# Six held pieces: when the long convolution's matmuls may be queued among the heads of the second mixer's attention

## The chip, the cores and the metric

One core of one Trainium2 chip runs the whole program. The metric is the device time of one execution in microseconds (us): 2259.91 us for the kernel before, the median of three runs (2259.61 to 2260.74). About 0.2% of it, 4.5 us, is what a measurement of this kernel can tell from no change.

## The reference, cut to what matters

The program is three transformer-like blocks in a row over 512 positions of width 1024. Only the middle of the second block is touched. There, one projection feeds two branches that don't depend on each other until their outputs are projected and added:

```
q = rope(rmsnorm(q)); k = rope(rmsnorm(k))            # 8 heads of 96
w = softmax(q @ k.T * 96**-0.5)                       # 512 x 512 per head
y_attn = w @ v                                        # 8 heads of 64

x0, x1, vh = split(dwconv3(u_h))                      # 3 x 512 channels
u = x1 * vh
y = irfft(rfft(u, 1024) * rfft(kcirc, 1024))[:512] + u * bias
y_hyena = x0 * y

x = x + concat(rmsnorm(y_attn), rmsnorm(y_hyena)) @ w_out
```

The kernel does the two transforms as matmuls with constant cosine and sine matrices. All large matmuls are done in three passes of split operands (high times high, low times high, high times low), so each weight tile is first cast to its high part on ScalarE and its low part is made by a subtraction on VectorE.

## The kernel before

The function is `mix2`. The position axis (512) is four tiles of 128. The program is written as one straight trace; a planner then orders it at compile time: it walks a simulated time line, lets every engine take the ready instruction that stands earliest in the trace, and fixes by that the order of each engine's queue. On the chip every queue runs in that order. Work that stands late in the trace but is ready early therefore fills holes of the work before it.

What stands where, in the order of the trace:

- Eight projections for the convolution's `x1` and `vh` (`uh`), with the norms of the attention's q and k between them, and the four products `us[i]`. `turned(i)` turns each product with four TensorE transposes into a bank of the tag `t`, and empties that bank by four pairs of a ScalarE copy (line 1484) and a VectorE subtraction (line 1485).
- `rotate` of q (lines 1375 to 1377), then `gate0(0)` and `gate0(1)`: each one projection of 24 matmuls and a three-tap convolution (line 268, 1283, 1285, 1286), stored for later. Then `turned(3)`.
- The attention. `heads(hd)` turns q and then k of one head (line 1582), into one `t` bank each, and empties the banks on ScalarE (line 211) and VectorE (line 212). `scores(hd)` makes four score tiles of three matmuls each in the two banks `s`, takes the row maximum on VectorE (line 1597) and the exponential on ScalarE (line 1599) into one of five buffers `P`. `values(hd)` turns the four `P` tiles, 16 transposes (line 1612, copied out by line 1614), and in every second head multiplies with v in the bank `o` and scales by the inverse sums.
- The six pieces of the list `fill`: `gate0(2)`, `gate0(3)`, `forward(0)`, `forward(1)`, `inverse(0)`, `inverse(1)`. A `forward` has 24 matmuls of 512 columns, mirrors them (lines 1273 to 1275), multiplies with the stored filter spectrum (lines 1526 to 1531 on VectorE and GpSimd), adds and subtracts (1535, 1536, GpSimd) and splits four results (202 and 204). Its eight buffers of the tag `tmp` are all that there are. An `inverse` has 48 matmuls of 256 columns and reads all eight split results of both forwards; then come line 1562 on VectorE, 1563 on GpSimd, and a split (211, 212).
- `hyena(n)`, eight output blocks of 12 matmuls each that read all of the convolution's result, and eight blocks `w2outa` that read all of the attention's. Those of `hyena` for n under 6 are held by `issue_after(marks[HOLD[n]])`.

The banks of the tag `t` are two, those of `mm` three; the cast weights have three buffers.

`marks` is a list of TensorE instructions. `mark()` appends the TensorE instruction traced last. It is called three times per head and once behind the loop:

```
            for hd in range(8):
                ...
                mark()
                pt = scores(hd, *qk, den)
                mark()
                if hd < 7:
                    qk = heads(hd + 1)
                mark()
                values(hd, pt, po, den)
            mark()
            for f in fill:
                f()
```

So `marks[3*hd]` is the last TensorE instruction ahead of the scores of head `hd`, `marks[3*hd + 1]` the last of its scores, and `marks[3*hd + 2]` the last transpose of the next head's k. `marks[0]` is the last transpose of the first head's k. `issue_after(ins)` makes every instruction of a block that runs on the engine of `ins`, here TensorE, stand behind `ins` in that engine's queue. It is an order of issue alone. Instructions of the block on other engines, and its DMAs, aren't held.

Of the kernel before, what the change touches and what calls it, by code (L numbers as in the profile page):

```python
# [1341 lines left out]
def mix2(k, h, r12, bc, kf, xp, x1, done):  # L1342
# [3 lines left out]
    with k.tc.tile_pool(name="m2", bufs=1) as p:  # L1346
# [125 lines left out]
        with k.tc.tile_pool(name="m2d", bufs=1) as pd:  # L1472
# [31 lines left out]
            def gate0(i):  # L1504
                t = uh(i)
                S.dma_start(out=sx0[i], in_=t)
# [8 lines left out]
            def forward(f):  # L1515
                w = k.w(k.aps["c_fw"][f])
                kk = [[tmp() for j in range(2)] for i in range(2)]
                for i in range(2):
                    for j in range(2):
                        S.dma_start(out=kk[i][j], in_=kf[j, 2 * f + i])  # L1520
                ab = [mirror(k, halves(k, w, j, un), tmp(), tmp()) for j in range(2)]
                m = []
                for i in range(2):
                    a, b, (k0, k1) = ab[0][i], ab[1][i], kk[i]
                    t = kk[0][1] if i else k.nm.tile([P, T], F32, tag="diag", bufs=1, name=k.name("ft"))
                    V.tensor_tensor(out=t, in0=a, in1=k0, op=ALU.mult)
                    V.tensor_tensor(out=k0, in0=b, in1=k0, op=ALU.mult)
                    G.tensor_tensor(out=a, in0=a, in1=k1, op=ALU.mult)
                    V.tensor_tensor(out=b, in0=b, in1=k1, op=ALU.mult)
                    G.tensor_tensor(out=t, in0=t, in1=b, op=ALU.subtract)  # L1530
                    G.tensor_tensor(out=a, in0=a, in1=k0, op=ALU.add)
                    m.append((t, a))
                for j in range(2):
                    x, y, d = m[0][j], m[1][j], kk[j][0]
                    G.tensor_tensor(out=d, in0=x, in1=y, op=ALU.subtract)
                    G.tensor_tensor(out=x, in0=x, in1=y, op=ALU.add)
                    for i, v in enumerate((x, d)):
                        n = 4 * i + 2 * j + f
                        Y[n] = k.split(k.A(n), v)
# [4 lines left out]
            def inverse(half):  # L1544
                ps = [k.bank(), k.bank()]
                for i in range(2):
                    hi, lo = k.w(k.aps["c_inv"][i])
                    for j in range(2):
                        c = 2 * half + j
                        o = ps[j][:, i * 256 : (i + 1) * 256]  # L1550
                        for f in range(4):
                            a, b = (y[:, c * P : (c + 1) * P] for y in Y[4 * i + f])
                            sl = slice(f * 256, (f + 1) * 256)
                            k.mm(o, a, hi[:, sl], f == 0, False)
                            k.mm(o, a, lo[:, sl], False, False)
                            k.mm(o, b, hi[:, sl], False, f == 3)
                for j in range(2):
                    c = 2 * half + j
                    u, x0 = tmp(), tmp()
                    S.dma_start(out=u, in_=su[c])  # L1560
                    S.dma_start(out=x0, in_=sx0[c])
                    V.scalar_tensor_tensor(out=u, in0=u, scalar=k.v("hbias", c), in1=ps[j], op0=ALU.mult, op1=ALU.add)
                    G.tensor_tensor(out=turns(x0), in0=halved(u), in1=turns(x0), op=ALU.mult)
                    u = x0
                    ym.append(k.split_scaled(B(c), u, k.v("onh", c)))
                    sq = tmp() if c else k.nm.tile([P, T], F32, tag="sqa", bufs=1, name=k.name("ha"))
                    S.activation(out=sq, in_=u, func=AF.Square)
                    if c:
                        V.tensor_tensor(out=hacc[0], in0=hacc[0], in1=sq, op=ALU.add)
                    else:  # L1570
                        hacc[0] = sq
# [31 lines left out]
            ya, marks = [], []  # L1603
# [38 lines left out]
            def inverse_sums(den):  # L1642
# [3 lines left out]
            fill = [  # L1646
                lambda: gate0(2),
                lambda: gate0(3),
                lambda: forward(0),
                lambda: forward(1),  # L1650
                lambda: inverse(0),
                lambda: inverse(1),
            ]
# [11 lines left out]
                mark()  # L1665
                values(hd, pt, po, den)
            mark()
            for f in fill:
                f()
            ws = {}  # L1670

            def out_half(nm, n, act, bank=("mm", 3)):
# [694 lines left out]
def build(tc, aps, out, vecmap):  # L2367
    with ExitStack() as ctx:
# [16 lines left out]
        drop()  # L2385
        nf2 = Norm(k, lambda i: k.v("norm_ffn_2", i), k.A)
        xs = mix2(k, h, n12.r, n12.bc, early.kf, xpool, n12.x1, nf2.add)
        h = nf2.finish()
        xa = []
# [83 lines left out]
```

## Time and profile before

| | us |
|---|---|
| median of three runs | 2259.91 |
| profiled execution | 2263.86 |
| its span, first to last instruction | 2262.1 |
| TensorE busy in the span | 2193.2 (97%) |
| VectorE busy | 1372.2 (61%) |
| ScalarE busy | 947.0 (42%) |
| GpSimd busy | 529.1 (23%) |

The profile is of one execution. The change lies between 788 us and 985 us of its span. A row of a table by stretches gives, for each engine, the busy time in the stretch and the number of instructions, then the mean granted clock of TensorE as a share of the full one, and the DMA's share. A row of a time line gives start, duration, engine, line, operation, output and inputs, and in brackets the idle time of the engine ahead of it and what ended it. Matmuls follow one another at about 0.23 us for 512 columns although each is shown as about 0.39 us long, because they overlap.

### The profile page before, as it was taken

To read this page: it belongs to the slowest core of one execution; us is meant where nothing else is said; L and a number is where in the kernel's file an instruction comes from. 1 tells how busy PE (TensorE), PEld (TensorE's weight loads), DVE (VectorE), ACT (ScalarE), POOL (GpSimd) and SP (SyncE) were. 2 spreads that over 40 slices of the span, in tenths; PEclk is the share of its full clock that TensorE was granted. 3 is DMA by queue.
4 is the path that set the end of the run, shared out by engine and by line. 5 is a ranking of instruction groups with operands and counts; after the bars stand their busy time and mean duration, and the time that the engine had idled before them with its cause. 6 is when DMAs were issued, how large, how long until landed. Compare 5 with 4: busy or idle time off the path is not lost.

```text
span 2262.1 us, 30194 instructions
## 1 busy us (share of the span) xinstructions
PE 2193.2 (97%) x11672; PEld 1793.4 (79%) x11672; DVE 1372.2 (61%) x2226; ACT 947.0 (42%) x1597; POOL 529.1 (23%) x454
## 2 busy tenths in 40 slices
PE   7898999999999998999999999999999999999998
PEld 4677788888888976688888886798888788888886
DVE  6564777753354598478647647877666754433333
ACT  4344556642243456544324434455544233222221
POOL 3233555521122225221001103000111221310220
PEclk7899999999999999999999999999999999999999
DMA  8552122224323342233232243222222422223322
GB/s 317 183 162 75 54 94 85 84 75 130 103 88 110 115 136 75 68 109 101 79 110 102 70 153 118 87 83 75 80 95 83 140 84 94 94 83 112 98 79 76
DMA packets 80728, 235.27 MB, mean 104 GB/s; under 512 B 9887, under 2 KB 10911, under 8 KB 80584
## 3 DMA queue, kind: packets, MB, share of 16 engines
q1 hardware_dynamic: 65768, 208.25, 28.2%
q10 hardware_dynamic: 14816, 25.08, 3.4%
q8 instruction: 92, 1.51, 0.3%
q14 instruction: 52, 0.43, 0.1%
HBM read 218.60 MB, written 15.22 MB: 103 GB/s over the span
## 4 chain that ended last, share of the span: by engine, by line
PE 56%; DVE 2%; issue 2%; ACT 1%; POOL 0%; POOLq 0%; DVEq 0%; ACTq 0%
PE mm L116 49%; PE s L116 3%; PE o L116 2%; PE t L116 1%; DVE sg L1772 0%; PE t L1612 0%; ACT wh L110 0%; DVE x L2438 0%; DVE st L1597 0%; DVE wl L111 0%; DVE x L1773 0%; DVE B L212 0%; PE t L2123 0%; ACT A L211 0%; PE t L2086 0%
## 5 line engine op out<-in xcount | busy, mean ns | idle before, releaser
L116 PE MATMUL mm<-A,wh 128*128 128x512 f32 x2176 | 691.1, 393 | 1.0 <-DVE A L212 1.0
L110 ACT CAST wh<-wr 128x1024 fp32r<-128x1024 f32 (+2 forms) x374 | 368.4, 987 | 609.6 <-PE mm L116 398.5
L111 DVE TENSOR_TENSOR wl<-wr,wh 128x1024 fp32r<-128x1024 f32 (+3 forms) x371 | 446.2, 1204 | 275.4 <-ACT wh L110 274.3
L116 PE MATMUL mm<-B,wh 128*128 128x512 f32 x1672 | 536.2, 396 | 1.3 <-DVE us L268 0.9
L116 PEld LDWEIGHTS mm<-A,wh 128*128 128x128 f32 x2176 | 409.6, 189 | 89.3 <-issue 1.9
L116 PE MATMUL mm<-A,wl 128*128 128x512 f32 x1088 | 425.8, 392 | 4.3 <-DVE wl L111 4.3
L116 PEld LDWEIGHTS mm<-B,wh 128*128 128x128 f32 x1672 | 313.5, 188 | 72.7 <-issue 4.0
L116 PE MATMUL mm<-B,wl 128*128 128x512 f32 x836 | 329.2, 394 | 0.0
L116 PEld LDWEIGHTS mm<-A,wl 128*128 128x128 f32 x1088 | 205.4, 189 | 47.7 <-DVE wl L111 6.3
L116 PEld LDWEIGHTS mm<-B,wl 128*128 128x128 f32 x836 | 157.3, 188 | 35.0 <-issue 3.0
L251 POOL TENSOR_TENSOR r<-r,mhalf 128x4 f32<-128x4 f32 (+1 forms) x40 | 53.2, 1332 | 407.6 <-DVE r L250 407.6
L116 PE MATMUL mm<-a,wh 128*128 128x512 f32 x448 | 140.5, 389 | 0.0
L268 DVE TENSOR_TENSOR us<-mm,bc 128x512 f32<-128x512 f32 x95 | 65.1, 688 | 97.2 <-PE mm L116 95.8
L204 POOL TENSOR_TENSOR a<-sl,a 128x512 fp32r<-128x512 f32 x28 | 40.5, 1446 | 274.2 <-ACT a L202 274.2
L116 PEld LDWEIGHTS mm<-a,wh 128*128 128x128 f32 x448 | 84.1, 188 | 17.5
L116 PE MATMUL mm<-a,wl 128*128 128x512 f32 x224 | 86.8, 389 | 0.0
L116 PE MATMUL mm<-wh,A 128*128 128x256 f32 x448 | 84.8, 285 | 0.0
L116 PEld LDWEIGHTS mm<-wh,A 128*128 128x128 f32 x448 | 71.0, 191 | 1.2 <-issue 0.6
L2358 POOL TENSOR_TENSOR sl<-sl,bc 128x512 f32<-128x512 f32 x22 | 28.7, 1305 | 167.6 <-DVE sl L1718 167.6
L116 PE MATMUL mm<-wl,A 128*128 128x256 f32 x224 | 63.6, 284 | 0.0
L116 PE MATMUL mm<-wh,B 128*128 128x256 f32 x320 | 61.2, 287 | 0.0
L1747 DVE TENSOR_TENSOR x<-x,mm 128x512 f32<-128x512 f32 x32 | 22.0, 687 | 64.5 <-PE mm L116 64.5
(588 smaller groups left out, 3472.0 us busy)
## 6 DMA issues: line engine op xcount, KB each, us to landing
wr<-w2upg SPq DMA_DIRECT2D x22, 512.0 KB, 3.4
wr<-w2upu SPq DMA_DIRECT2D x22, 512.0 KB, 3.4
wr<-w3fg SPq DMA_DIRECT2D x22, 512.0 KB, 3.4
wr<-w3fu SPq DMA_DIRECT2D x22, 512.0 KB, 3.4
adar<-w1ada SPq DMA_DIRECT2D x16, 512.0 KB, 7.6
wr<-w3out SPq DMA_DIRECT2D x16, 512.0 KB, 3.5
wr<-w1ib SPq DMA_DIRECT2D x14, 512.0 KB, 3.5
wr<-w2uh SPq DMA_DIRECT2D x12, 512.0 KB, 3.4
```

The lines of the kernel that those rows point to most:

```text
L110: nc.scalar.copy(out=hi[:, :n], in_=r[:, :n])
L111: (eng or nc.vector).tensor_tensor(out=lo[:, :n], in0=r[:, :n], in1=hi[:, :n].bitcast(F32), op=ALU.subtract)
L116: return self.nc.tensor.matmul(out, a, b, start=start, stop=stop)
L204: eng.tensor_tensor(out=l[:p], in0=src, in1=hi[:p].bitcast(F32), op=ALU.subtract)
L251: nc.gpsimd.tensor_tensor(out=r, in0=r, in1=self.mhalf[:, :n], op=ALU.pow)
L268: self.nc.vector.tensor_tensor(out=out, in0=ps, in1=bc, op=ALU.mult)
L1747: k.nc.vector.tensor_tensor(out=xs[n], in0=xs[n], in1=ps, op=ALU.add)
L2358: nc.gpsimd.tensor_tensor(out=s, in0=s, in1=norm.bc, op=ALU.mult)
```

## The change

Each of the six pieces is traced inside an `issue_after` of its own. The numbers are indices of `marks`.

```
-            for f in fill:
-                f()
+            for f, m in zip(fill, (0, 3, 5, 11, 16, 18)):
+                with k.tc.issue_after(marks[m]):
+                    f()
```

By the rule for the marks above, and with heads counted from zero: `gate0(2)` stands behind the transposes of head 0's k, `gate0(3)` behind the last transposes of head 0's `P`, `forward(0)` behind the transposes of head 2's k (traced inside head 1), `forward(1)` behind those of head 4's k (inside head 3), `inverse(0)` behind the scores of head 5, and `inverse(1)` behind the last value matmuls of head 5. Nothing else of the program is edited; `HOLD` stays (0, 0, 15, 18, 21, 24).

## Rows read from the trace of the kernel before

**Rows 1.** The page: the span, the busy row of TensorE, and the granted clock in 40 slices of the span, in tenths.

```profile
span 2262.1 us, 30194 instructions
...
PE 2193.2 (97%) x11672; PEld 1793.4 (79%) x11672; DVE 1372.2 (61%) x2226; ACT 947.0 (42%) x1597; POOL 529.1 (23%) x454
...
PEclk7899999999999999999999999999999999999999
```

**Rows 2.** The table by stretches, whole core: the stretch, its length, busy time and instructions of TensorE, its weight loads, VectorE, ScalarE and GpSimd, then granted clock, DMA share and GB/s.

```profile
788.00:818.40 30.40, 30.40 (x140) 25.13 (x139) 29.34 (x52) 14.74 (x27) 13.81 (x7) 1.00 0.31 108
818.40:834.30 15.90, 15.90 (x79) 13.15 (x78) 14.83 (x24) 8.20 (x15) 0.00 (x0) 1.00 0.56 191
834.30:848.20 13.90, 12.88 (x63) 9.63 (x62) 12.81 (x19) 6.63 (x15) 4.44 (x4) 1.00 0.39 122
848.20:888.00 39.80, 32.13 (x148) 20.19 (x148) 37.26 (x49) 26.93 (x57) 24.04 (x17) 0.87 0.21 66
888.00:956.00 68.00, 64.61 (x373) 47.63 (x371) 37.14 (x52) 39.90 (x78) 16.59 (x12) 1.00 0.19 63
956.00:984.40 28.40, 28.40 (x132) 23.27 (x131) 22.36 (x25) 12.97 (x19) 12.79 (x8) 1.00 0.45 149
```

**Rows 3.** The waits of TensorE between 834.3 us and 888 us, the longest sum: waiter, releaser, us in total, times, longest.

```profile
PE s L116 <- ACT P L1599: 5.1, 5, 3.3
```

**Rows 4.** The groups of VectorE between 834.3 us and 888 us that belong to the forward transforms: busy us, mean ns of one, idle time before them.

```profile
L204 DVE TENSOR_TENSOR A<-tmp,A 128x512 fp32r<-128x512 f32 x6 | 6.0, 1002 | 0.6 <-ACT A L202 0.6
L1527 DVE TENSOR_TENSOR tmp<-tmp,tmp 128x512 f32<-128x512 f32 x4 | 4.5, 1116 | 0.0
L1529 DVE TENSOR_TENSOR tmp<-tmp,tmp 128x512 f32<-128x512 f32 x4 | 3.8, 946 | 0.0
...
L1526 DVE TENSOR_TENSOR tmp<-tmp,tmp 128x512 f32<-128x512 f32 x2 | 2.9, 1460 | 0.1
L1274 DVE TENSOR_TENSOR tmp<-tmp,mm 128x512 f32<-128x512 f32 x4 | 2.7, 682 | 1.2 <-DMA scr_x<-tmp 1.0 <-PE mm L116 0.3
L1275 DVE TENSOR_TENSOR tmp<-tmp,mm 128x512 f32<-128x512 f32 x4 | 2.7, 677 | 0.0
...
L1526 DVE TENSOR_TENSOR ft<-tmp,tmp 128x512 f32<-128x512 f32 x2 | 1.4, 690 | 0.0
L204 DVE TENSOR_TENSOR A<-ft,A 128x512 fp32r<-128x512 f32 x2 | 1.4, 688 | 0.1
```

**Rows 5.** TensorE's time line around the entry to the attention: the last turned product, the first head's q, the first head's k, the first scores.

```profile
818.81 0.60 PE L1479 MATMUL t<-ident,tmp 128*128 128x128 f32 x4
...
823.38 0.60 PE L1582 MATMUL t<-ident,q 128*96 128x128 f32 x4
...
831.63 0.60 PE L1582 MATMUL t<-ident,k 128*96 128x128 f32 x4
...
834.37 0.63 PE L116 MATMUL s<-kT,qT 96*128 96x512 f32 x2
```

**Rows 6.** TensorE's groups between 818.4 us and 831.4 us, the two largest: projections of the `A` operands.

```profile
L116 PE MATMUL mm<-A,wh 128*128 128x512 f32 x30 | 10.0, 398 | 0.0
L116 PE MATMUL mm<-A,wl 128*128 128x512 f32 x15 | 5.8, 390 | 0.0
```

**Rows 7.** VectorE's time line at the entry: the end of the rotation, the convolution and weight split of the later pieces, and the last subtraction that empties the bank of the last turned product.

```profile
820.62 0.68 DVE L1377 TENSOR_TENSOR q<-tmp,tmp 128x512 f32<-128x512 f32 x1
...
825.99 0.68 DVE L268 TENSOR_TENSOR tmp<-mm,bc 128x512 f32<-128x512 f32 x1
826.59 0.28 DVE L1485 TENSOR_TENSOR B<-t,B 128x128 fp32r<-128x128 f32 x1
826.92 1.23 DVE L111 TENSOR_TENSOR wl<-wr,wh 128x1024 fp32r<-128x1024 f32 x1
...
828.72 0.74 DVE L1285 SCALAR_TENSOR_TENSOR tmp<-tmp,vec,tmp 128x511 f32<-128x511 f32 x1
829.38 0.28 DVE L1485 TENSOR_TENSOR B<-t,B 128x128 fp32r<-128x128 f32 x1
```

**Rows 8.** Three idle holes of TensorE, each in the first instruction behind it: two inside the attention, one in the first block.

```profile
256.79 1.50 PE L116 MATMUL s<-qk 128*64 128x64 f32 x24 [4.37 <-DVE qk L847]
...
854.07 0.50 PE L116 MATMUL s<-kT,qT 96*128 96x512 f32 x1 [1.40 <-ACT kT L211]
...
877.61 0.96 PE L116 MATMUL s<-kT,qT 96*128 96x512 f32 x3 [3.33 <-ACT P L1599]
```

**Rows 9.** The table by stretches around these three holes, columns as in the second group.

```profile
852.00:862.00 10.00, 8.57 (x39) 5.32 (x40) 8.89 (x13) 8.23 (x18) 6.11 (x5) 0.83 0.26 81
874.00:890.00 16.00, 12.16 (x51) 7.62 (x50) 13.62 (x19) 8.61 (x19) 10.21 (x7) 0.79 0.21 67
252.00:266.00 14.00, 9.63 (x77) 8.12 (x76) 12.75 (x20) 8.26 (x12) 10.38 (x13) 0.63 0.22 76
```

**Rows 10.** TensorE's time line in the later heads: the first solid run of an inverse, the first output block of the convolution, the last scores of head 5, the last value matmuls of head 5.

```profile
888.95 0.28 PE L116 MATMUL mm<-wh,A 128*128 128x256 f32 x1
...
904.48 0.39 PE L116 MATMUL mm<-B,wh 128*128 128x512 f32 x1
...
911.38 0.96 PE L116 MATMUL s<-kT,qT 96*128 96x512 f32 x3 [0.44 <-ACT P L1599]
...
929.63 1.94 PE L116 MATMUL o<-pT,v 128*64 128x512 f32 x8 [0.31 <-DVE pT L1614]
```

## The prediction

> **What bounds the kernel now.** I read the page first: TensorE is busy 97% of the span [rows 1], so a gain can only come from the 3% and from the clock. The table by stretches says where these lie around the change [rows 2]. From 788 us to 834.3 us TensorE has no idle time at all, and VectorE is busy 44.17 of 46.3 us: two engines are full at once. From 834.3 us the attention runs. TensorE idles 13.90 - 12.88 = 1.02 us to 848.2 us, 39.80 - 32.13 = 7.67 us to 888 us, and 68.00 - 64.61 = 3.39 us to 956 us; the 28.4 us behind it are full. VectorE is busy 37.26 of 39.80 us in the second of these stretches and only 37.14 of 68.00 us in the third. The middle is VectorE's, the rest TensorE's. The reader should see two neighbouring stretches with opposite limits.
>
> The waits give the mechanism [rows 3]: scores wait 5.1 us for a bank that an exponential has to empty, and the exponential stands behind a row maximum in VectorE's queue. What fills that queue is the two forwards [rows 4]: 6.0 + 4.5 + 3.8 + 2.9 + 2.7 + 2.7 + 1.4 + 1.4 = 25.4 us, 12.7 us each, and 17.2 us of it lie in four groups whose mean is 0.95 to 1.46 us where others of the same shape take 0.69 us. Both come together because their matmuls ran before and in head 0, as filling that the engine didn't need there.
>
> The clock costs too. In 848.2 to 888 us the granted clock is 0.87 [rows 2], so 39.8 x 0.13 = 5.2 us of full-speed time are lost; it falls behind idle holes [rows 8, 9].
>
> **The change, term by term.** The matmuls stay, one for one: 4 x 24 of 512 columns and 2 x 48 of 256. Only their places in TensorE's queue change, so the sum is one of idle time and clock. I make it against the profiled execution, 2263.86 us; the median is 3.95 us lower.
>
> *What can go.* 1.02 + 7.67 + 3.39 = 12.1 us of idle time and 5.2 us of clock: 17.3 us at most.
>
> *What comes at the entry.* This is the term that the diff doesn't show. `marks[0]` is head 0's k, turned at 831.63 us [rows 5]. From 818.4 us, where `gate0(1)` ends, to there TensorE runs the projections of `gate0(2)` and `gate0(3)`, 45 matmuls in these two rows [rows 6], then the first of `forward(0)`. Nearly all of that must now stand behind k, and nothing else is ready. What is left ahead of k are two groups of transposes, `turned(3)` and head 0's q [rows 5], 0.60 us each. k itself waits for a bank `t`: the two are used in turn, so k takes the one of `turned(3)`, whose last subtraction starts at 829.38 us and lasts 0.28 us [rows 7]. VectorE then sheds three instructions that hang on held matmuls: line 268 at 825.99 (0.60 us to the next start), the split at 826.92 (1.23 us), which waits for a buffer that a held piece now keeps, and line 1285 at 828.72 (0.66 us to the next start): 2.4 us, as starts overlap a little [rows 7]. So the bank is free at about 829.7 - 2.4 = 827.3 us, and TensorE is empty for 827.3 - 818.4 - 1.2 = 7.7 us. Bounds: q needs the rotation, which ends at 821.3 us [rows 7]; were the bank free by then, k would follow q at 821.9 us and the hole were 2.3 us. With k where it is now, 831.6 us, it is 12.0 us. I take 7.7 us, since it is the present order with what leaves it taken out.
>
> *The clock behind that hole.* Behind holes of 1.40, 3.33 and 4.37 us [rows 8] the deficits are 10 x 0.17 = 1.7, 16 x 0.21 = 3.4 and 14 x 0.37 = 5.2 us [rows 9], part of them inside the hole, where they cost nothing. The first is followed by dense 512-column matmuls, as `gate0(2)` will be; I take 1.7 us, bounds 0 and 5.2.
>
> *What stays idle in the heads.* Head 0 keeps one piece of 24 x 0.23 = 5.5 us as filling and loses VectorE's share of the forwards: 1.0 us, as now. Heads 1 to 3 carry one forward instead of two, half of 7.67 or 3.8 us, and they carry `gate0(3)` and `forward(0)` as new filling; I halve it once more, 1.9 us. `forward(1)` moves its 12.7 us of VectorE work into heads 3 to 5, where nothing is released until head 5 is scored, and its own 24 matmuls are all the cover: between 1.9 and 3.8 us, 2.7. From there the inverses fill as they do now: 3.0 of the 3.39 us. Together 8.6 us, bounds 5 (each of the middle terms 0.5) and 12.1 (as before). The clock falls once more there, behind the hole of head 4: 1.7 us, bounds 0 and 5.2.
>
> *What costs nothing.* The casts, splits and loads of the pieces aren't held, but with three cast buffers they follow the pieces that free them; SP's queue behind them holds only weights of still later work, so it waits unseen. The spectrum loads of `forward(0)` need `tmp` buffers that `gate0(3)` gives back late. They are issued from ScalarE's queue, with exponentials behind them; if the planner's order puts them too early, ScalarE stands, which I leave inside the 8.6 us. GpSimd's queue holds only the forwards' and inverses' own products here. `hyena(0)` to `hyena(3)` follow the inverses into head 7 and the 28.4 full microseconds behind the heads: the same work in the same row, later.
>
> **Sum:** -12.1 - 5.2 + 7.7 + 1.7 + 8.6 + 1.7 = +2.4 us, 2266.3 us for a profiled execution, and 2259.91 + 2.4 = 2262.3 us for the median: no change that can be told.
>
> [...] TensorE's weight loads are busy 23.27 of 28.40 us (82%) in the full stretch, but 9.63 of 13.90, 20.19 of 39.80 and 47.63 of 68.00 us in the three of the attention [rows 2]. [...]
>
> **The rivals.**
>
> *A, the planner closes the hole (faster).* The planner sees TensorE empty at 818 us and orders ScalarE and VectorE for the bank: hole 2.3 us, its clock 1.7, and the spread works as meant, 5 us left in the heads with no further fall of the clock: -17.3 + 2.3 + 1.7 + 5.0 = -8.3, or 2251.6 us. For it: four subtractions of 0.28 us, with a copy ahead of each, end 10.9 us behind the transposes at 818.81 us only because other work lies between [rows 5, 7]; and VectorE has 30.9 us to spare from 888 to 956 us [rows 2]. Against it: VectorE is full at the entry [rows 2], and the convolutions of `gate0(0)` and `gate0(1)` stand earlier in the trace than the attention.
>
> *B, the entry decides (slower).* k stays at 831.6 us because VectorE's queue closes up with other splits: hole 12.0 us and the large clock deficit, 5.2: -17.3 + 12.0 + 5.2 + 8.6 + 1.7 = +10.2, or 2270.1 us. For it: VectorE is busy without a break to there. Against it: three of its instructions go. It decides once hole and clock exceed my 9.4 us by 2.1, thus from a k later than about 829.4 us.
>
> *C, the inverses come too late (slower).* They start at 888.95 us now, output blocks at 904.48 us; they'd start behind the scores of head 5 (911.38 us now) and behind its last value matmuls (929.63 us) [rows 10], and all `hyena` blocks wait for both. If the last two heads then stand bare twice, each a hole as the longest in the attention, 3.33 us [rows 8], it is +2.4 + 6.7 = +9.1, or 2269.0 us. Against it: 48 matmuls of the second inverse lie in just that place.
>
> *D, the holds don't bind.* All six marks lie behind where the pieces run now [rows 5, 10], so this is nearly excluded: 2259.9 us.
>
> **Chances.** Forecast 0.38, A 0.27, B 0.27, C 0.05, D 0.03. What a measurement here can tell from no change is 0.2%, 4.5 us. So faster 0.27, same 0.38 + 0.03 = 0.41, slower 0.27 + 0.05 = 0.32. The forecast alone would have 2257 to 2264 us; A and B hold more than half of the chance, so the range runs past A's and B's own values, 2250 to 2271 us, and leaves out about 2 in 10.
>
> **What would show it.** A hole of TensorE of 6 to 10 us between 818 and 828 us, ended by the transposes of head 0's k, with a granted clock near 0.5 behind it: else the entry term is wrong. The first scores at about 829 instead of 834.4 us. VectorE's two forwards apart, heads 1 to 3 with under 4 us idle, and no single wait for an exponential of 3 us there; a new hole in head 4. First output block of the convolution behind head 6. If the hole is under 4 us, A holds; if it is over 10, B; if waits of 3 us and more stand in heads 6 and 7, C.

## The result, and the profile after

The changed kernel takes 2269.38 us (median of six runs, 2267.86 to 2271.18) against 2259.76 us for the kernel before, measured beside it: ratio 1.005, with a 95% interval of 1.0036 to 1.0063 (the ratio is taken over the runs; that of the two medians is 1.0043). It is slower by 9.6 us, and that is more than the 0.2% that can be told. The forecast was 2262.3 us, no change.

The page of the changed kernel, its span, the busy row of TensorE and the granted clock:

```profile
span 2269.4 us, 30196 instructions
...
PE 2195.4 (97%) x11672; PEld 1794.2 (79%) x11672; DVE 1373.1 (61%) x2226; ACT 947.1 (42%) x1597; POOL 528.7 (23%) x454
...
PEclk8899999999999999999999999999999999999999
```

Beside [rows 1] it has the same counts of instructions on each of these engines, and TensorE's busy time differs by 2.2 us. The page can't say where 9.6 us went; the table by stretches can. First the changed kernel, columns as in [rows 2]. Its line numbers behind the edit are one higher than before's.

```profile
784.00:814.90 30.90, 30.90 (x141) 25.52 (x140) 29.44 (x55) 14.51 (x28) 14.37 (x8) 1.00 0.33 111
814.90:830.80 15.90, 9.77 (x34) 7.50 (x33) 10.44 (x17) 4.78 (x9) 0.91 (x1) 0.68 0.30 100
830.80:848.30 17.50, 16.10 (x85) 12.59 (x84) 10.58 (x16) 10.32 (x24) 0.00 (x0) 1.00 0.13 45
848.30:903.40 55.10, 47.31 (x236) 30.93 (x235) 50.66 (x68) 36.16 (x75) 30.73 (x21) 0.97 0.31 91
903.40:960.50 57.10, 53.83 (x298) 39.15 (x296) 31.97 (x42) 30.65 (x59) 15.24 (x12) 0.94 0.22 69
960.50:992.60 32.10, 32.10 (x148) 26.18 (x147) 22.67 (x25) 13.12 (x19) 10.91 (x8) 1.00 0.43 141
```

Length less TensorE's busy time is its idle time: 15.90 - 9.77 = 6.13 us at the entry, where before had none, and 1.40 + 7.79 + 3.27 = 12.46 us within the heads, where before had 12.08 [rows 2]. Length times what the clock lacks is what the clock takes at most: 15.9 x 0.32 + 55.1 x 0.03 + 57.1 x 0.06 = 5.1 + 1.7 + 3.4 = 10.2 us, where before had 5.2. So 6.5 us more idle time and 5.0 us more clock: up to 11.5 us. Part of the entry's 5.1 us of clock lies inside the hole and costs nothing. The same stretch in three parts (last product of the convolution to first scores; the heads, to the end of the last value matmuls; what is left up to the next block's first matmul), first before, then after:

```profile
814.24:834.37 20.13, 20.13 (x98) 16.60 (x97) 19.06 (x28) 9.02 (x15) 3.79 (x2) 1.00 0.49 167
834.37:956.10 121.73, 109.65 (x582) 77.52 (x580) 87.15 (x118) 73.39 (x149) 45.08 (x32) 0.96 0.22 70
956.10:984.46 28.36, 28.36 (x131) 23.18 (x131) 22.42 (x25) 13.04 (x19) 12.79 (x8) 1.00 0.45 149
```

```profile
811.75:830.80 19.05, 12.92 (x48) 10.08 (x47) 13.59 (x21) 4.78 (x9) 3.77 (x2) 0.73 0.29 97
830.80:960.70 129.90, 117.44 (x616) 82.78 (x615) 93.21 (x124) 77.13 (x154) 45.98 (x32) 0.96 0.25 76
960.70:992.52 31.82, 31.82 (x145) 25.98 (x146) 22.59 (x25) 13.04 (x19) 10.91 (x8) 1.00 0.43 140
```

The entry is 1.1 us shorter though TensorE has half as many instructions in it (48 against 98); the heads are 8.2 us longer, and what follows is 3.5 us longer. Together 180.77 - 170.22 = 10.6 us. (The spans of the two profiled executions differ by only 7.3 us; the stage begins 2.5 us earlier in the changed one, and there the programs are alike. Executions of one kernel scatter by some us, so single stages are read here to about that, and totals by the ratios alone.)

TensorE at the entry of the changed kernel, beside [rows 5]:

```profile
814.92 0.60 PE L1479 MATMUL t<-ident,tmp 128*128 128x128 f32 x4
818.82 1.09 PE L1582 MATMUL t<-ident,q 128*96 128x128 f32 x4 [3.30 <-DVE q L1377]
822.74 1.09 PE L1582 MATMUL t<-ident,k 128*96 128x128 f32 x4 [2.83 <-DVE qT L212]
...
824.48 1.05 PE L116 MATMUL mm<-A,wh 128*128 128x512 f32 x2
...
829.88 0.63 PE L116 MATMUL mm<-A,wh 128*128 128x512 f32 x2
...
830.80 1.53 PE L116 MATMUL s<-kT,qT 96*128 96x512 f32 x6
```

Two holes instead of one: 3.30 us until the rotation has written q, 2.83 us until the bank of k is free. Behind the first of them the granted clock is 0.50, the lower level (1.2 of 2.4 GHz), in every microsecond from 819 to 828: a transpose group takes 1.09 us instead of 0.60, and a pair of projections 1.05 instead of 0.63 us until about 828.6 us. And 21 projections of `gate0(2)` stand between k and the first scores. VectorE over the same time, beside [rows 7]:

```profile
818.09 0.68 DVE L1377 TENSOR_TENSOR q<-tmp,tmp 128x512 f32<-128x512 f32 x1
...
821.95 0.74 DVE L212 SCALAR_TENSOR_TENSOR qT<-t,gs,qT 96x512 fp32r<-96x512 f32 x1
...
825.34 0.28 DVE L1485 TENSOR_TENSOR B<-t,B 128x128 fp32r<-128x128 f32 x1
831.91 0.69 DVE L1597 TENSOR_REDUCE st<-s 128x1 f32<-128x512 f32 x1 [6.29 <-PE s L116]
```

k follows the instruction that empties q's bank (821.95 us); the last subtraction of `turned(3)` ends at 825.6 us, 2.9 us behind k's transposes. So k takes q's bank, not that of `turned(3)`, as [rows 7] had been read. VectorE, the engine said to be full here, then stands 6.29 us until the scores come.

The longest waits of TensorE within the heads, from the first scores to the last value matmuls, first before, then after:

```profile
PE s L116 <- ACT P L1599: 5.6, 6, 3.3
PE o L116 <- DVE pT L1614: 1.2, 2, 0.9
PE t L1612 <- DVE qT L212: 0.3, 1, 0.3
```

```profile
PE s L116 <- ACT P L1599: 3.0, 4, 1.1
PE t L116 <- DVE hr L296: 2.9, 2, 1.9
PE o L116 <- DVE pT L1614: 1.3, 2, 1.0
PE t L1612 <- DVE qT L212: 1.2, 2, 0.9
```

The waits for exponentials did shrink, and the 3.3 us one is gone. Others have come in their place: 2.9 us for the chain of the inverse sums (line 296), which has no row in the list of before, and 1.2 instead of 0.3 us for the next head's q. The copies of the turned `P` cost the same in both. Nor did VectorE's instructions of the forwards get shorter on the whole by lying apart; two groups, beside [rows 4]:

```profile
L204 DVE TENSOR_TENSOR A<-tmp,A 128x512 fp32r<-128x512 f32 x6 | 7.3, 1215 | 0.1
L1526 DVE TENSOR_TENSOR tmp<-tmp,tmp 128x512 f32<-128x512 f32 x2 | 2.1, 1035 | 0.1
```

The first was 6.0 us, 1002 ns each; the second was 2.9 us, 1460 ns each. The four slow groups of [rows 4] together take 18.3 us, where they took 17.2.

### The profile page after: what moved, and what is told of

It reads as the page before. It is cut to its first block, busy times and chain, and to the rows that moved or that the text cites. A ratio compares the mean times of both kernels' runs of the same rounds, so it can differ in the third digit from the quotient of the medians.

```text
span 2269.4 us, 30196 instructions
## 1 busy us (share of the span) xinstructions
PE 2195.4 (97%) x11672; PEld 1794.2 (79%) x11672; DVE 1373.1 (61%) x2226; ACT 947.1 (42%) x1597; POOL 528.7 (23%) x454
## 4 chain that ended last, share of the span: by engine, by line
PE 56%; DVE 2%; issue 2%; ACT 1%; POOL 0%; DMA 0%; POOLq 0%; DVEq 0%; ACTq 0%
PE mm L116 49%; PE s L116 3%; PE o L116 2%; PE t L116 1%; DVE sg L1773 0%; DVE x L1774 0%; DVE x L2439 0%; PE t L1612 0%; ACT wh L110 0%; DVE A L204 0%; DMA tmp<-scr_x 0%; ACT B L211 0%; ACT A L211 0%; PE t L2124 0%; DVE wl L111 0%
## 5 line engine op out<-in xcount | busy, mean ns | idle before, releaser
L116 PEld LDWEIGHTS mm<-a,wh 128*128 128x128 f32 x448 | 84.1, 188 | 17.4
```

The costliest lines, as they stand in the source:

```text
L116: return self.nc.tensor.matmul(out, a, b, start=start, stop=stop)
```

## The experiments

Three theories were at hand for the loss. The hole: idle time at the entry and the half clock behind it. The late pieces: forwards or inverses released too late leave heads bare or the end long. And one that took shape on the way: the heads have no room at all, so a loose matmul (one of the convolution or an output block, as against those of the heads themselves) costs its whole time wherever in the heads it stands; the expectations call it theory 3 and, in the last two, the serial theory.

Nearly all experiments change the tuple of marks alone, and leave some pieces without a hold:

```diff
-            for f, m in zip(fill, (0, 3, 5, 11, 16, 18)):
-                with k.tc.issue_after(marks[m]):
+            for f, m in zip(fill, (None, None, 5, 11, 16, 18)):
+                with k.tc.issue_after(marks[m]) if m is not None else ExitStack():
                     f()
```

This table holds what was measured in all of them. "Holds" is the tuple, with - for None. "Loose" is the loose matmuls within the heads, counted in the table of groups, at 0.2325 us for 512 columns (nine follow each other in 2.09 us in the full stretch of before) and 0.119 us for 256. "Heads" runs from the first scores to the end of the last value matmuls. The columns "idle" and "clock" are of the heads alone; clock is the length times what the granted clock lacks of 1, and as that is printed to two digits, the column is good to some 0.6 us. "Own" is heads less loose, idle time and clock. All in us, from the one profiled execution; the ratio is to the kernel before as measured beside that run, with its interval.

| run | holds | entry | idle in it | heads | loose | idle | clock | own | ratio |
|---|---|---|---|---|---|---|---|---|---|
| before | none | 20.1 | 0 | 121.7 | 36.8 | 12.1 | 4.9 | 67.9 | 1 |
| after | 0,3,5,11,16,18 | 19.1 | 6.1 | 129.9 | 43.7 | 12.5 | 5.2 | 68.5 | 1.0050 (1.0036 to 1.0063) |
| e1 | -,-,5,11,16,18 | 18.3 | 2.2 | 125.2 | 37.9 | 12.6 | 6.3 | 68.4 | 1.0010 (0.9998 to 1.0023) |
| e2 | 0,3,-,-,-,- | 18.0 | 6.6 | 139.9 | 47.2 | 14.3 | 12.6 | 65.8 | 1.0058 (1.0043 to 1.0073) |
| e3 | as after, filled | 17.4 | 2.0 | 123.5 | 35.8 | 17.5 | 1.2 | 69.0 | 1.0045 (1.0028 to 1.0062) |
| e4 | -,-,-,11,-,- | 20.1 | 0 | 128.5 | 36.8 | 14.7 | 9.0 | 68.0 | 1.0038 (1.0019 to 1.0057) |
| e5 | as after, k first | 17.2 | 6.1 | 132.3 | 44.2 | 12.5 | 6.6 | 69.0 | 1.0050 (1.0034 to 1.0065) |
| e6 | -,3,5,11,16,18 | 16.5 | 4.9 | 132.6 | 43.0 | 13.3 | 9.3 | 67.0 | 1.0041 (1.0029 to 1.0054) |
| e7 | -,-,5,11,-,- | 18.3 | 2.2 | 126.3 | 41.0 | 13.5 | 3.8 | 68.0 | 1.0017 (1.0005 to 1.0029) |
| e8 | -,-,-,-,16,18 | 20.1 | 0 | 111.2 | 25.8 | 14.8 | 2.2 | 68.4 | 1.0016 (1.0002 to 1.0029) |
| e9 | all 24 | 13.0 | 7.0 | 80.5 | 0 | 9.1 | 2.4 | 69.0 | 1.0261 (1.0246 to 1.0277) |
| e10 | none; blocks at 24 | 20.1 | 0 | 107.4 | 18.6 | 14.5 | 8.6 | 65.7 | 1.0044 (1.0030 to 1.0058) |
| e11 | -,3,-,-,-,- | 16.5 | 4.9 | 133.3 | 46.5 | 12.4 | 6.7 | 67.7 | 1.0041 (1.0029 to 1.0054) |
| e12 | 0,-,-,-,-,- | 19.0 | 6.1 | 128.3 | 47.2 | 12.5 | 1.3 | 67.3 | 1.0027 (1.0016 to 1.0037) |
| e13 | 1,3,5,11,16,18 | 13.0 | 7.0 | 133.4 | 48.6 | 11.6 | 5.3 | 67.9 | 1.0037 (1.0025 to 1.0050) |
| e14 | -,-,-,5,-,- | 20.1 | 0 | 126.6 | 36.8 | 15.1 | 6.3 | 68.4 | 1.0037 (1.0024 to 1.0049) |

**Which holds carry the loss (e1, e2).** The first of the two new lines (e1) leaves the two gates unheld, the second (e2) holds them alone:

```diff
-            for f, m in zip(fill, (0, 3, 5, 11, 16, 18)):
+            for f, m in zip(fill, (None, None, 5, 11, 16, 18)):
+            for f, m in zip(fill, (0, 3, None, None, None, None)):
```

> The two gate pieces are released as in the kernel before, the forwards and inverses stay held as in the changed one. Theory 1 (the entry: what was lost is the hole ahead of head 0's k and the half clock behind it, 6.1 us idle and up to 5.1 us of clock; the spread inside the heads won nothing, 12.5 us idle and 5.1 us of clock against 12.1 and 5.2): no hole of over 2 us between 810 and 830 us, full clock there, and a time within 4 us of the kernel before. Theory 2 (the heads: late forwards and inverses cost, and the gates are the only cover that heads 0 and 1 have): still 6 us or more slower than before, with new idle time in heads 0 and 1.

> Only the two gate pieces are held, forwards and inverses as before. Theory 1: the hole stays, since the forwards need the last turned product too, so 5 us or more idle between 814 and 830 us with half clock behind it, and 6 to 11 us slower than before. Theory 2: heads 0 and 1 have more cover than before and nothing comes late, so within 4 us of before or faster, hole or not.

Without the gates' holds +0.10%, not to be told from no change; with them alone +0.58%, the whole loss (12.9 us by the medians, where theory 1 had at most 11). The place is the gates. But the hole at the entry of e2 (6.6 us) is hardly larger than that of the changed kernel (6.1), while its heads idle and lose clock for 26.9 us against 17.7, so one number doesn't make the price.

**Fill the hole with unread work (e3), or shorten it (e5).** The first adds 23 matmuls whose result nobody reads, ahead of q and of k of head 0, so that TensorE doesn't go idle there. The second turns head 0's k ahead of its q; mark 0 is then the transposes of q.

```diff
+            def spin(n):
+                d = k.bank("o", 1)
+                with k.tc.issue_after(k.last_pe()):
+                    for i in range(n):
+                        k.mm(d, h[i % 8][0][:, :P], h[0][0], True, True)
...
+                    if hd == 0:
+                        spin(13 if nm == "qT" else 10)
```

```diff
-                for x, g, nm in ((qh, gs, "qT"), (kt, k.v("gk"), "kT")):
+                for x, g, nm in ((qh, gs, "qT"), (kt, k.v("gk"), "kT"))[:: 1 if hd else -1]:
...
-                return res
+                return res if hd else res[::-1]
```

> The changed kernel with 23 matmuls more, of 512 columns, whose results nobody reads: 13 ahead of head 0's q and 10 between its q and its k, 23 x 0.23 = 5.3 us laid into the 6.1 us hole. If the clock behind the hole is a cost of its own: full clock from 815 to 831 us, the first gate piece takes 5.5 instead of 7.1 us, and the kernel is 2 to 4 us faster than the changed one, thus 6 to 8 us slower than before. If the clock is only a sign of the hole and the chain ahead of the scores sets the time: no gain, 9 to 12 us slower than before.

> The changed kernel with one order swapped: head 0 turns k ahead of q. k's data are ready 20 us before q's, so the mark on which the first gate piece waits becomes q's last transpose, behind the rotation, and no longer a second transpose that needs a bank of its own. Theory 1 (the hole at the entry sets the loss): the hole is 3 to 4 us instead of 6.1, the half clock behind it shorter, and the kernel 3 to 5 us faster than the changed one, thus 4 to 7 us slower than before. Theory 2 (the chain of the first scores sets it, not TensorE's hole): q is ready no earlier, so no gain over the changed kernel, 8 to 12 us slower than before.

The two stretches of e3, the entry and the heads up to the last value matmuls:

```profile
805.74:823.16 17.42, 15.47 (x73) 12.25 (x72) 13.61 (x21) 4.79 (x9) 3.78 (x2) 1.00 0.31 106
823.16:944.76 121.60, 104.13 (x574) 74.87 (x572) 90.05 (x122) 75.84 (x150) 39.77 (x29) 0.99 0.23 74
```

Since the hole is filled with work of no use, only what the clock takes could come back. The clock is full, 1.00 and 0.99, and its loss falls from 10.2 us to 1.2; yet the median is only 2.3 us lower than that of the changed kernel, and the intervals overlap. The heads now idle 17.5 us instead of 12.5: much of what the clock gave back, TensorE spent waiting within the heads; why the idle time rose there was not separated. e5 changes nothing: the hole is still 6.1 us. So the clock behind the hole is not the main part of its price; what remains is that no useful matmul ran in it.

**One hold at a time (e4, e6, e7, e8, e11, e12).** Holds as in the table.

> Only the second forward is held, at the mark of the changed kernel (inside head 3). VectorE's 12.7 us of its products leave heads 1 to 3, the entry is as before. Theory 1: no hole at the entry; heads 1 to 3 idle less than now, but the inverses wait for the second forward and heads 4 and 5 idle more: within 4 us of before, either side. Theory 2: 5 us or more slower, from heads 4 and 5.

> All holds of the changed kernel but that of the first gate piece, which may again fill the entry with its 5.5 us. Theory 1: the hole falls from 6.1 to about 1 us, clock full, gate0(3) is cover for head 1: within 4 us of before, or faster by up to 6 us if the spread was worth something once the entry is closed. Theory 2 (the second gate piece in head 1 costs too): 5 us or more slower than before.

> Only the two forwards are held; gates and inverses as before. If the inverses' own holds cost nothing, this equals the kernel with gates free, within 3 us of it (about +2 us against before). If they cost by baring heads 4 and 5, this is 3 us or more faster than that kernel. If holding them is what gains, 3 us or more slower.

> Only the two inverses are held, behind the scores of head 5 and the value matmuls of head 5; gates and forwards as before. If late inverses cost: heads 3 to 5 stand bare, the idle time there rises by 3 to 8 us over before, and the kernel is 3 to 8 us slower. If they don't: within 3 us of before, since the same matmuls lie in heads 6 and 7.

> Only the second gate piece is held: 24 matmuls, 5.6 us, go from the entry into head 1. Theory 3: at the entry VectorE's chain takes its 17 us or more whatever TensorE does, so the place there was free, and in head 1 the piece costs its full time: 4 to 8 us slower than before, with the hole at the entry 3 us or more. Theory 1 as first put (a long hole and its half clock): gate0(2) fills most of the entry, so under 3 us slower.

> Only the first gate piece is held, behind head 0's k; the second may fill the entry in its place, being one of the same size that is ready as early. If what counts is how much work the entry keeps: 4 to 8 us slower than before, as with only the second one held, since one of the two is gone from it. If it is the hold of gate0(3) in head 1 that costs, within 3 us of before.

Each gate costs by itself (`gate0(3)` +0.41%, `gate0(2)` +0.27%). So does `forward(1)` alone (e4, +0.38%; one of its twelve runs took 2287.53 us at a granted clock of 0.916, and the medians give +0.27%), without any hole at the entry, while both forwards together cost +0.17% and the inverses +0.16%, both under the 0.2% that can be told. The single prices add up to far more than the whole, so they are no terms of a sum. Three expectations missed: in e6 the hole was to fall to about 1 us and stayed at 4.9, since k still waits for q's bank; e11 was to cost 4 to 8 us and cost 9.4 by the medians; and e4's new idle time lies in head 0 (3.7 us instead of 1.0) as well as in heads 4 and 5, where it was expected. And none of the arrangements has less idle time in the heads than before, but for 0.5 us in e13 and for e9, which has no loose work there.

**What the heads are without any loose work (e9), and without output blocks (e10).** In e9 all six pieces and all blocks stand behind the last head (the first tuple below); in e10 the blocks alone do, and no piece is held (the second).

```diff
-HOLD = (0, 0, 15, 18, 21, 24)
+HOLD = (24, 24, 24, 24, 24, 24)
...
-            for f, m in zip(fill, (0, 3, 5, 11, 16, 18)):
+            for f, m in zip(fill, (24, 24, 24, 24, 24, 24)):
+            for f, m in zip(fill, (None, None, None, None, None, None)):
```

> All six pieces and all held output blocks stand behind the last head, so that the heads run bare. Measured from the first scores to the last value matmuls, less the time of the loose matmuls in between, the heads took 83.0 us before and 84.2 us in the changed kernel. Theory 3 (a chain: the heads need some 84 us of their own and each loose matmul between them adds its whole time, because it stands in the same queue ahead of the chain's next step): the bare heads take 80 to 90 us. Theory of cover (loose matmuls fill holes that are there anyway, as the forecast had it): bare they take over 95 us, with 25 us or more idle. Either way the entry hole is 6 us and the kernel 10 us or more slower than before.

> The kernel before with its output blocks all held behind the last head: some 60 matmuls of 512 columns, 14 us, leave heads 4 to 7 for the full stretch behind. Theory 3: it costs them as much time there as they leave free here, within 4 us of before. Theory of cover: heads 5 to 7 stand bare and idle 8 us or more, the kernel 6 us or more slower.

The three parts of e9:

```profile
812.75:825.70 12.95, 5.98 (x27) 4.21 (x25) 12.67 (x20) 4.55 (x9) 3.77 (x2) 0.77 0.35 115
825.70:906.20 80.50, 71.36 (x365) 43.03 (x365) 45.24 (x70) 52.03 (x117) 2.75 (x2) 0.97 0.01 5
906.20:1038.80 132.60, 91.83 (x416) 75.20 (x416) 76.76 (x83) 40.29 (x57) 60.61 (x40) 0.82 0.33 107
```

This is the run that says most. Bare heads take 80.5 us, of which TensorE is busy 71.4, and idle 9.1. That is all that there was to fill, and with 36.8 us of loose work in the kernel before the idle time isn't less: there the heads are 41.2 us longer and idle 12.1 us. The reader should also see the first row, where a bare entry takes 12.95 us with VectorE busy 12.67 and TensorE idle 7.0: that is where loose matmuls can be had for nothing. The last row is where e9 loses its 57 us: the pieces' own chain, TensorE idle 40.8 us in two holes of 12.6 and 13.2 us and many small ones. So the loose matmuls don't fill holes of the heads; the heads fill holes of the pieces.

The parts of e10:

```profile
805.08:825.20 20.12, 20.12 (x98) 16.60 (x96) 19.04 (x28) 8.98 (x15) 3.79 (x2) 1.00 0.47 162
825.20:932.60 107.40, 92.95 (x488) 63.20 (x486) 84.19 (x115) 68.52 (x141) 37.68 (x26) 0.92 0.23 71
932.60:983.10 50.50, 50.06 (x225) 40.97 (x224) 25.80 (x30) 18.61 (x27) 24.39 (x16) 0.97 0.32 104
```

Loose work is 18.2 us less, the heads 14.3 us shorter; idle time and clock take 6.1 us of it back, and the total is slower by 0.44%. Theory 3 had it within 4 us of before (0.18%), so here it missed, and the total came as the theory of cover said, though heads 5 to 7 idle 5.8 us and not 8. So the whole time isn't quite what a loose matmul costs: with less of them the clock is lower, 0.92 against 0.96.

**Two last ones (e13, e14).** What stayed open was whether the lump of projections ahead of the first scores is the price, or its matmuls wherever they stand; and whether the forwards apart, without any hold at the entry, lower the idle time at all. The first new line is e13, the second e14.

```diff
-            for f, m in zip(fill, (0, 3, 5, 11, 16, 18)):
+            for f, m in zip(fill, (1, 3, 5, 11, 16, 18)):
+            for f, m in zip(fill, (None, None, None, 5, None, None)):
```

> The changed kernel with gate0(2) one mark later, behind the scores of head 0 instead of behind its k, so that its 24 matmuls no longer stand between k and the first scores. Serial theory (a loose matmul within the heads costs its whole time; the bare heads' own chain is about 80 us and the entry from the last product to the first scores about 13 us when nothing stands in it): the entry falls from 19.0 to 13 or 14 us, the loose matmuls within the heads rise by 5.6 us, idle in the heads stays between 11 and 15 us; the total gets only what the half clock took from those 24 matmuls, ratio 1.002 to 1.005. Rival, the lump ahead of the first scores is what costs: the 6 us come back whole, ratio under 1.002. Rival, the clock gate: the hole is followed at once by the sparse matmuls of the scores, the clock in the heads falls further, ratio over 1.006.

> The kernel before with one hold alone: forward(1) behind the transposes of head 2's k, some 20 us later than it ran, so that VectorE gets its 12.7 us apart from those of forward(0). Spreading theory (the reason for the forecast's gain): idle time in the heads falls below 9 us, no wait for an exponential over 1.5 us, ratio 0.996 to 0.999. Serial theory (bare heads idle 9.1 us already, and every arrangement tried had 12 to 15): idle in the heads 11 to 15 us, the loose matmuls within the heads unchanged at about 37 us, ratio 0.9995 to 1.004.

The parts of e13, and the start of its heads:

```profile
806.09:819.05 12.96, 5.99 (x27) 4.21 (x25) 12.68 (x20) 4.55 (x9) 3.79 (x2) 0.77 0.33 115
819.05:952.50 133.45, 121.87 (x636) 88.39 (x637) 94.50 (x126) 77.83 (x155) 44.84 (x32) 0.96 0.24 77
952.50:984.30 31.80, 31.80 (x146) 26.00 (x147) 22.14 (x25) 13.03 (x19) 10.85 (x8) 1.00 0.43 139
```

```profile
817.09 1.09 PE L1582 MATMUL t<-ident,k 128*96 128x128 f32 x4 [2.82 <-DVE qT L212]
819.05 2.92 PE L116 MATMUL s<-kT,qT 96*128 96x512 f32 x6 [0.88 <-ACT kT L211]
```

The scores now follow k in 2.0 us, the entry is the bare one of e9 to 0.01 us (12.96), and the heads are 3.6 us longer than in the changed kernel for 4.9 us more of loose work. Of the 6.1 us won at the entry 3.6 are paid back; the ratio fell from 1.0050 to 1.0037, and the intervals overlap. So the lump ahead of the scores is at most a small part of the price; most of it comes with its matmuls, wherever they stand. For e14 the three parts, and its longest wait:

```profile
805.17:825.29 20.12, 20.12 (x97) 16.60 (x96) 19.05 (x28) 8.96 (x15) 3.79 (x2) 1.00 0.48 163
825.29:951.90 126.61, 111.50 (x582) 78.74 (x580) 86.96 (x118) 74.03 (x149) 47.72 (x32) 0.95 0.22 68
951.90:980.60 28.70, 28.69 (x131) 23.21 (x132) 23.19 (x25) 13.06 (x19) 12.18 (x8) 1.00 0.45 147
```

```profile
PE s L116 <- ACT P L1599: 3.3, 3, 1.5
```

The forwards lie apart, the loose work is the same 36.8 us, the long wait for an exponential is halved, and the idle time is 15.1 us, not under 9; the ratio, 1.0037, lies near the upper end of what the serial theory allowed. Spreading the forwards moves the waits and doesn't remove them. No version that was tried is faster than the kernel before.

## Why the prediction was wrong

The step that failed is the gain in the heads. The prediction had 12.1 + 5.2 us of idle time and clock shrink there to 8.6 + 1.7, a gain of 7.0 us; measured are 12.5 + 5.1, a loss of 0.3. The entry was forecast to cost 7.7 + 1.7 = 9.4 us and cost 6.1 + 5.1 = 11.2.

The table shows the same in every run. "Own" is what TensorE needs for the heads' own matmuls, which are the same in all runs but for a few small ones, so that it stays at 66 to 69 us checks the sums and explains nothing. What counts is that idle time and clock take 11.5 us (e9) to 27 us (e2) on top, 17.0 in the kernel before and 17.7 after. The gain needed these 17.0 us to shrink. So the heads cost neither less nor much more than before, beside the loose work that came into them. What the change added is at the entry: 6.1 us in which no useful matmul runs, and a lower clock behind. The matmuls that filled those microseconds run in the heads instead, where they cost their time. Idle time and clock of entry and heads together are 17.0 us before, 28.9 after and 26.9 in e13 (the clock of their entries is 0.73 and 0.77): 11.9 and 9.9 us more, where the ratios say 11.3 and 8.4. The variants without a hold on the gates pay otherwise: e4, e10 and e14 have a full entry, and lose 21 to 24 us to idle time and clock in the heads.

- *Idle left in the heads, 8.6 us: this step failed.* Measured 12.5 us. By heads, first before (head 0, heads 1 to 3, heads 4 to 7), then after (head 0, heads 1 to 3, head 4, heads 5 and 6, head 7):

```profile
834.37:845.31 10.94, 9.94 (x47) 7.56 (x46) 9.94 (x16) 5.03 (x11) 2.56 (x2) 1.00 0.47 151
845.31:881.31 36.00, 28.64 (x143) 18.71 (x143) 34.54 (x44) 23.85 (x51) 22.25 (x16) 0.92 0.18 59
881.31:956.10 74.79, 71.07 (x395) 51.25 (x395) 42.66 (x60) 44.51 (x88) 20.27 (x15) 0.97 0.20 64
```

```profile
830.80:837.80 7.00, 5.60 (x31) 4.06 (x29) 5.15 (x8) 5.16 (x11) 0.00 (x0) 1.00 0.00 0
837.80:880.89 43.09, 39.23 (x194) 28.00 (x194) 34.83 (x48) 26.05 (x54) 14.90 (x10) 0.96 0.31 98
880.89:896.31 15.42, 12.79 (x68) 7.16 (x66) 14.22 (x21) 8.69 (x19) 8.74 (x6) 1.00 0.24 69
896.31:925.52 29.21, 26.57 (x172) 20.45 (x173) 24.08 (x31) 20.99 (x42) 11.48 (x9) 1.00 0.24 73
925.52:960.70 35.18, 33.26 (x160) 23.12 (x159) 14.93 (x20) 16.24 (x31) 10.85 (x9) 0.90 0.22 69
```

  In the changed kernel length less busy time is 1.4, 3.9, 2.6, 2.6 and 1.9 us, where the forecast had 1.0 for head 0, 1.9 for heads 1 to 3, 2.7 for heads 3 to 5 and 3.0 behind. So the halving of 7.67 us for the forward taken out came true: heads 1 to 3 idle 3.9 us, where before had 7.4. The second halving, for the matmuls moved there as filling, did not. And heads 4 to 7 idle 7.2 us, where before had 3.7: what heads 1 to 3 won, the later heads lost. The kernel e7, where the two forwards alone are held, has the same (3.3 and 8.2 us). Of the 3.9 us above the forecast 2.0 lie in heads 1 to 3, 1.5 in heads 4 to 7 (7.2 against 2.7 + 3.0) and 0.4 in head 0. The bare heads idle 9.1 us without any forward, so 8.6 was less than the heads by themselves leave, and e14 shows the idle time rising when the forwards are spread. The bound at the other end, "12.1 (as before)", was the value.
- *What can go, 12.1 + 5.2 us.* Read rightly as idle time and clock; as something that can go it was not. "The middle is VectorE's" rested on 37.26 of 39.80 us [rows 2], but in the bare heads VectorE is busy only 45.24 of 80.50 us, and TensorE idles 9.1 us all the same.
- *The entry's hole, 7.7 us.* Measured 3.30 + 2.83 = 6.1 us. The size was nearly right, but by luck, since the working was not: it put all of it ahead of k and had k wait for the bank of `turned(3)`. It waits for q itself and then for q's bank. That the work in `gate0(2)` and `gate0(3)` was cover at this place, and that the diff doesn't show it, was the right step of the prediction: e9 and e13 show 7.0 us of bare idle time there, which the kernel before fills wholly.
- *The clock behind that hole, 1.7 us: mis-sized.* Measured 15.9 x 0.32 = 5.1 us, about the upper bound (5.2). Dense projections did follow, but they ran at the lower level until 828.6 us, 5.6 us long. In e3, with the clock held up, the median is 2.3 us lower.
- *The clock in the heads, 1.7 us: mis-sized.* 1.7 + 3.4 = 5.1 us, again the upper bound (5.2). The forecast had one fall of the clock there.
- *What costs nothing.* The queues of SP and GpSimd weren't seen to hold anything back; no wait on a DMA or on GpSimd is in TensorE's list of the heads.

With what was measured the sum is -12.1 - 5.2 + 6.1 + 5.1 + 12.5 + 5.1 = +11.5 us, against a stage longer by 10.6 us and a median higher by 9.6. Of the 9.1 us between this and the forecast, 3.9 come from the idle time in the heads, 3.4 from each clock, and the entry gave 1.6 back.

Of the rivals, B's time (2270.1 us) was right within 0.8 us, but by luck, and not B: k didn't stay where it was, and the hole is not over 10 us. Nor is it A: the planner did bring k forward, but not to a hole of 2.3 us, and nothing was won in the heads. C is ruled out for this kernel by its waits: none of 3 us in heads 6 and 7. D fell with the first row that moved.

Of "what would show it", the clock near 0.5 behind the hole, the forwards apart and the missing 3 us wait came true. The first scores came 19.05 us behind the last product instead of 20.13, some 4 us later than forecast, since 21 projections ran ahead of them, most at half rate, which the forecast counted as work and not as a delay of the scores. Heads 1 to 3 do idle under 4 us (3.86), and the first output block runs behind the scores of head 6. The new hole in head 4 didn't come as one: its 2.6 us are in pieces of about 1 us.

The busy share of the weight loads fares worse than the idle time as a measure of room. The Trainium skill (Perfetto Trace Analysis, "Identifying the Most-Contended Engine") says to judge TensorE's headroom by MFU, the share of the peak rate that its matmuls reach, and by the busy share of the weight loads. In the bare heads weight loads are busy 43.03 of 80.50 us. Held against the 82% of the full stretch [rows 2], they would leave room for 0.82 x 80.5 - 43.0 = 23 us (an estimate that takes the full stretch for the limit). The idle time says 9.1 us. The kernel before has 36.8 us of loose work in its heads, and they are longer by 41.2, so even the idle time told too much.

What stays open is which step of the softmax chain makes the 12 to 15 us: the waits go over from one link to the next (exponential, inverse sums, next head's q) with each arrangement. It also stays open why one forward held alone (e4, e14) seems to cost more than both together (e7). Each arrangement has one profiled execution, so differences of 1 or 2 us in idle time say little. That a planned order of single matmuls, rather than pieces held by a mark, could bring the heads to the 9.1 us of e9 wasn't tried.

## What to carry to other kernels

Before spreading filling over a stage, run the stage bare: its idle time then bounds what filling can win in the stage itself, and here it was 9.1 of 80.5 us, of which no arrangement won anything. Ask of each piece of filling what it covers where it stands now: an engine that idles 0% because of the filling will idle when it leaves. And a wait that disappears from the list of waits is no gain until the idle time of the stretch has fallen; compare the sum, not the longest line.

## What was not expected of the hardware

- Matmuls that only hold the clock up (e3: granted clock 0.99 in the heads instead of 0.96) were worth little: the idle time there rose by 5.0 us as the clock's loss fell by about 4.
- VectorE's slow instructions of the forwards don't get shorter on the whole when the two forwards lie apart: 18.3 us in the four groups against 17.2 before, and 1215 ns each in the largest group against 1002, where others of the shape take 0.69 us [rows 4]. What lengthens them was not separated.
- The bare entry is the same to 0.01 us in two kernels (12.95 and 12.96 us), while whole executions of one kernel scatter by some 10 us (28 of before, from 2251.08 to 2262.84 us).
